# Attention's output kept by channels, and three head groups mixed at once: one change to a hybrid decoder block

## The chip, the cores and the metric

The kernel runs on one core of a Trainium2 chip. The metric is the device time of one execution in microseconds (us). The kernel before took 1356.09 us in the median of three runs, 1356.03 to 1356.96.

A core has engines with instruction rows of their own: TensorE (PE in the profile, with its weight loads as PEld), VectorE (DVE), ScalarE (ACT), GpSimd (POOL) and SyncE (SP), which here issues nearly all transfers. An engine runs its row in order, and waits on semaphores for what others have to finish first. Matmuls read the on-chip memory and write PSUM banks; ScalarE and VectorE carry PSUM out, which is called an eviction here.

## The reference

One layer of a decoder block, on 1024 positions of 1024 channels, in float32:

```python
h = rms_norm(x, mix_norm_g[layer])
proj = h @ w_in[layer]
z_a, q, k, v, gate_logits = jnp.split(proj, splits, axis=-1)
y_a = chunked_spatial_gating(gelu(z_a), ...)
...
y_b = dilated_mixture_attention(q, k, v)
gates = jax.nn.sigmoid(...)
merged = gates[:, :, 0] * (y_a @ w_branch_a) + gates[:, :, 1] * (y_b @ w_branch_b)
x = x + merged @ w_out[layer]
...
```

A convolutional gated MLP with `w_up` and `w_down` and a final norm follow. The change is in `dilated_mixture_attention`. There are three groups of four heads, 64 channels each. A group attends within a window, over every position, every 4th or every 16th. Each head gives an output and a log-sum of its exponentials for each position. The three groups are then mixed, head by head, by a softmax over the three log-sums:

```python
alpha = jax.nn.softmax(jnp.stack(lses, axis=-1), axis=-1)
mixed = jnp.einsum('bshg,bshgd->bshd', alpha, o_all)     # (1024, 256)
```

## The kernel before

**Input products.** The first long stage computes `h @ w_in` channel-major (channels on the partitions, positions along a row). It goes through 23 blocks of 256 output columns, held in `PAIRS`: three of v for the gating (zv), then for each head group, in the order 1, 2, 0, three blocks (qa, qc, v), then gate blocks ga 0 to 3, three u blocks (zu 0 to 2), and gate blocks ga 4 to 7. A block is done by seven products of half size, a scheme that trades a product for sums, in the order P1, P6, P2, P7, P5, P4, P3 (`in_order`, L326). Each product is 12 matmuls (`in_product`, L533). P2 adds into P1's PSUM bank, P4 into P7's and P3 into P5's (`SHARED`, L528). `in_evict` (L559) carries each product out: P6 at L574, P7 at L579, P5 at L581, P4 at L584 and P3 at L587, all on VectorE; P1 and P2 on ScalarE. So P4 cannot start before L579 has read P7's bank, nor P3 before L581 has read P5's.

A product's weights are raw loads (wr), summed on VectorE (L277 to L282) and split into a high part on ScalarE (L312) and a low part on VectorE (L313); `in_ahead` keeps that four products ahead and the loads nine.

**What lies between.** Small work is put between the products by a clock of ticks: `after(lag, fn)` notes a function, and `in_product` calls `tick()` after every six matmuls. TensorE's row is therefore as the code writes it. The rows of the other engines and of SP are ordered by the framework's scheduler from product 18 on, which may place an instruction earlier than the code has it; once placed, the row runs in order.

**Attention.** When a group's v block is done, `attention` (L999) turns v to position-major (`turn_v`, two 128-position transposes per block of positions), and starts eight tiles of 128 queries, five ticks apart. A tile (`Attend`, L813) loads q and k, splits them into a high and a low part (`turn`), computes scores against its own key block and, where there is one, the block before it (`score`; one block in 13 tiles, two in the other 11), takes the exponentials, transposes the probabilities (`turn_p`, pp) and multiplies them with v (`product`, pu). In before, the probabilities are the weights and 64 value channels stream past, so the output has queries on the partitions.

For groups 1 and 2 the product and its two statistics (negative maximum and denominator, four heads each) go to a scratch in DRAM, 264 numbers a row. For group 0 `combine` (L938) loads the rows of the other two, forms the three shares with a dozen small VectorE operations, scales and adds on VectorE and GpSimd, and five ticks later `turn_y` transposes the result (ybt) into YC, channel-major.

**Around it.** From zu 0 on, `wd_load` and `wd_sums` (L1060, L1068) prepare the weights of the last stage: in each of eleven steps four quarters of `w_down` are loaded, four subtractions and additions are made on VectorE (L1076), and the results are stored. There are two buffers for each quarter. In before a step comes at P1 and at P5 of each block from zu 0 on. Each zu block also multiplies u by the mixed gating values (L673). In the last block, ga 7, `y_parts` (L1080) splits the gating output ya and the attention output YC into high and low parts in R, 8 of each after P6 and 8 after P7, for the products that follow.

Of the kernel before, what the change touches and what calls it, by code (L numbers as in the profile page):

```python
# [11 lines left out]
F32 = mybir.dt.float32  # L12
# [26 lines left out]
UW = NH * HD + 2 * NH  # L39
# [55 lines left out]
def block_kernel(  # L95
# [116 lines left out]
    def after(lag, fn):  # L212
        pending.setdefault(clock[0] + lag, []).append(fn)
# [590 lines left out]

    scratch = {g: dram.tile([S, UW], F32, name=f"scr{g}") for g in (1, 2)}

# [6 lines left out]
    class Attend:  # L813
# [6 lines left out]
        def __init__(self, g, T, vts):  # L820
            self.g, self.T, self.vts = g, T, vts
# [31 lines left out]
        def score(self):  # L853
# [14 lines left out]
            st = at.tile([P, UW], F32, name=f"st_{name}", tag="st", bufs=2)  # L868
            mx = small.tile([P, NH], F32, name=f"mx_{name}", tag="mx")
            pr_t = at.tile([P, NH, 256], F32, name=f"pr_{name}", tag="pr", bufs=2)  # L870
# [23 lines left out]
            nm = st[:, 256 : 256 + NH]  # L894
            den = st[:, 256 + NH : 256 + 2 * NH]
# [6 lines left out]
            self.st, self.pr = st, pr_t  # L902
# [17 lines left out]
        def product(self):  # L920
            pu = ps_x.tile([P, 256], F32, name=f"pu_{self.name}", tag="pu")
            n = len(self.parts)
            for i, (h, s) in enumerate(self.blocks):
                vt = self.vts[self.halves[s]]
                nc.tensor.matmul(  # L925
                    pu[:, h * HD : (h + 1) * HD],
                    self.pT[:, i, :],
                    vt[:, h * HD : (h + 1) * HD],
                    start=i % n == 0,
                    stop=i % n == n - 1,  # L930
                )
            if self.g != 0:
                nc.vector.tensor_copy(self.st[:, 0:256], pu)
                nc.sync.dma_start(scratch_rows(self.g, self.T), self.st)
            else:
                self.combine(pu)

        def combine(self, pu):  # L938

            T, st = self.T, self.st  # L940
            others = []
            for g in (1, 2):
                t = at.tile([P, UW], F32, name=f"ld_{g}_{T}", tag=f"ld{g}", bufs=1)
                nc.sync.dma_start(t, scratch[g][T * P : (T + 1) * P, :])
                others.append(t)
            srcs = [st] + others
            nms = [t[:, 256 : 256 + NH] for t in srcs]
            dens = [t[:, 256 + NH : 256 + 2 * NH] for t in srcs]
            w = small.tile([P, 3, NH], F32, name=f"w_{T}", tag="w", bufs=2)
            nmin = small.tile([P, NH], F32, name=f"nmin_{T}", tag="nmin", bufs=2)  # L950
            z = small.tile([P, NH], F32, name=f"z_{T}", tag="z", bufs=2)
            wd = small.tile([P, 3, NH], F32, name=f"wd_{T}", tag="wd", bufs=2)
            nc.vector.tensor_tensor(nmin, nms[1], nms[2], ALU.min)
            nc.vector.tensor_tensor(nmin, nmin, nms[0], ALU.min)
            for g in range(3):
                nc.vector.tensor_tensor(w[:, g, :], nmin, nms[g], ALU.subtract)
            nc.scalar.activation(w, w, AF.Exp)
            for g in range(3):
                nc.vector.tensor_tensor(wd[:, g, :], w[:, g, :], dens[g], ALU.mult)
            nc.vector.tensor_tensor(z, wd[:, 0, :], wd[:, 1, :], ALU.add)  # L960
            nc.vector.tensor_tensor(z, z, wd[:, 2, :], ALU.add)
            nc.vector.reciprocal(z, z)
            zb = z.unsqueeze(1).to_broadcast([P, 3, NH])
            nc.vector.tensor_tensor(w, w, zb, ALU.mult)  # L964

            def v4(ap):
                return ap.rearrange("p (h d) -> p h d", h=NH)

            def wb(g):
                return w[:, g, :].unsqueeze(2).to_broadcast([P, NH, HD])  # L970

            yb = st[:, 0:256]
            nc.vector.tensor_tensor(v4(yb), v4(pu), wb(0), ALU.mult)
            for g in (1, 2):
                o = others[g - 1]
                nc.gpsimd.tensor_tensor(v4(o[:, 0:256]), v4(o[:, 0:256]), wb(g), ALU.mult)  # L976
                nc.gpsimd.tensor_tensor(yb, yb, o[:, 0:256], ALU.add)
            after(5, self.turn_y)

        def turn_y(self):  # L980
            pt = tr_tile(f"ybt_{self.T}")
            for c in range(2):
                nc.tensor.transpose(
                    pt[:, c * P : (c + 1) * P], self.st[:, c * P : (c + 1) * P], ident
                )
            nc.scalar.activation(
# [1525 lines left out]
```

## Time and profile before

| | before |
|---|---|
| device time, median of three runs | 1356.09 us |
| span of the profiled execution, first to last instruction | 1355.9 us |
| mean granted TensorE clock | 0.998 |
| TensorE busy | 1345.9 us, 99% |
| VectorE busy | 1038.0 us, 77% |
| ScalarE busy | 642.0 us, 47% |
| GpSimd busy | 302.2 us, 22% |
| VectorE, 420 to 440 us | 18.17 of 20 us, DMA share 0.93 |

The span and the median run are 0.2 us apart. A line of the timeline is: start, duration of the run of equal instructions, engine, line of the kernel, operation, output<-inputs, shape, count. A float32 matmul (pu, pm) is two instructions; a transpose is one. Matmuls overlap, so durations of neighbours add up to more than their starts are apart. Attention's tiles lie from about 148 to 400 us, the u blocks from about 412 us, and the gate block ga 7 ends at 545.5 us.

### The profile page before, as it was taken

To read this page: it belongs to the slowest core of one execution; us is meant where nothing else is said; L and a number is where in the kernel's file an instruction comes from. 1 tells how busy PE (TensorE), PEld (TensorE's weight loads), DVE (VectorE), ACT (ScalarE), POOL (GpSimd) and SP (SyncE) were. 2 spreads that over 40 slices of the span, in tenths; PEclk is the share of its full clock that TensorE was granted. 3 is DMA by queue.
4 is the path that set the end of the run, shared out by engine and by line. 5 is a ranking of instruction groups with operands and counts; after the bars stand their busy time and mean duration, and the time that the engine had idled before them with its cause. 6 is when DMAs were issued, how large, how long until landed. Compare 5 with 4: busy or idle time off the path is not lost.

```text
span 1355.9 us, 19084 instructions
## 1 busy us (share of the span) xinstructions
PE 1345.9 (99%) x6356; PEld 1120.5 (83%) x6356; DVE 1038.0 (77%) x1894; ACT 642.0 (47%) x1269; POOL 302.2 (22%) x302
## 2 busy tenths in 40 slices
PE   9999999999999999999999999999999999999998
PEld 8888888888888878888888888888888888888886
DVE  7988697887877988769779878666666668585674
ACT  7763455665543325435366344333433335354453
POOL 1121000001330000210010346555655553000002
PEclk9999999999999999999999999999999999999999
DMA  9435454554438994975651223333233328996663
GB/s 356 112 99 172 130 171 118 149 156 140 135 110 295 324 324 144 300 263 164 236 170 39 67 105 105 98 117 114 89 116 118 124 92 269 387 332 221 201 205 124
DMA packets 144802, 236.99 MB, mean 175 GB/s; under 512 B 13888, under 2 KB 58432, under 8 KB 144704
## 3 DMA queue, kind: packets, MB, share of 16 engines
q1 hardware_dynamic: 142464, 231.79, 51.9%
q0 software_dynamic: 1088, 2.10, 0.9%
q10 hardware_dynamic: 1152, 1.89, 0.4%
q8 instruction: 50, 0.82, 0.3%
q14 instruction: 48, 0.39, 0.1%
HBM read 167.77 MB, written 64.29 MB: 171 GB/s over the span
## 4 chain that ended last, share of the span: by engine, by line
PE 90%; DVE 4%; DMA 3%; POOL 1%; issue 1%; ACT 1%; SPq 0%; POOLq 0%; DVEq 0%; ACTq 0%
PE in_P L544 22%; PE uP L1952 21%; PE dn L2215 15%; PE up L1952 8%; PE wo_P L1784 6%; PE pa L1414 5%; PE pl L617 3%; PE pu L925 2%; PE pu L1932 2%; PE pb L1414 2%; DMA wd<-in_w_down_dram 2%; DMA wT<-wd 1%; PE pp L909 1%; DVE wd L1076 1%; DVE G L313 1%
## 5 line engine op out<-in xcount | busy, mean ns | idle before, releaser
L544 PE MATMUL in_P<-R,G 128*128 128x512 f32 x1008 | 243.8, 394 | 0.0
L544 PEld LDWEIGHTS in_P<-R,G 128*128 128x128 f32 x1008 | 185.8, 188 | 36.9
L2215 PE MATMUL dn<-R 128*128 128x512 f32 x924 | 209.6, 389 | 0.0
L2215 PEld LDWEIGHTS dn<-R 128*128 128x128 f32 x924 | 173.5, 188 | 35.9
L544 PE MATMUL in_P<-G,G 128*128 128x512 f32 x504 | 123.3, 395 | 1.4 <-DVE C L579 1.4
L170 ACT ACTIVATE R<-up 128x512 fp32r<-128x512 f32 x109 | 65.7, 622 | 123.2 <-DVE up L279 105.9
L1952 PE MATMUL uP<-G,R 128*128 128x512 f32 x504 | 121.4, 390 | 0.0
L1952 PE MATMUL uP<-R 128*128 128x512 f32 x504 | 121.2, 390 | 0.0
L312 ACT ACTIVATE G<-wr 128x512 fp32r<-128x512 f32 x126 | 78.7, 628 | 89.5 <-PE in_P L544 51.4
L1952 PE MATMUL up<-G,R 128*128 128x512 f32 x504 | 120.3, 390 | 0.0
L1952 PEld LDWEIGHTS uP<-G,R 128*128 128x128 f32 x504 | 94.5, 188 | 20.1 <-DVE R L171 0.3
L1952 PEld LDWEIGHTS up<-G,R 128*128 128x128 f32 x504 | 94.7, 188 | 19.7
L1952 PEld LDWEIGHTS uP<-R 128*128 128x128 f32 x504 | 94.7, 188 | 19.6
L544 PEld LDWEIGHTS in_P<-G,G 128*128 128x128 f32 x504 | 92.8, 188 | 21.0 <-issue 2.6
L313 DVE TENSOR_TENSOR G<-wr,G 128x512 fp32r<-128x512 f32 x126 | 88.2, 701 | 25.2 <-ACT G L312 24.3
L171 POOL TENSOR_TENSOR R<-up,R 128x512 fp32r<-128x512 f32 x55 | 73.2, 1343 | 13.1 <-ACT R L170 12.2
L170 ACT ACTIVATE R<-db 128x512 fp32r<-128x512 f32 x77 | 48.1, 626 | 55.0 <-PE dn L2215 42.7
L171 DVE TENSOR_TENSOR R<-db,R 128x512 fp32r<-128x512 f32 x77 | 53.9, 704 | 25.0 <-ACT R L170 24.9
L1414 PE MATMUL pa<-R,G 128*128 128x512 f32 x288 | 67.9, 389 | 0.0
L1414 PEld LDWEIGHTS pa<-R,G 128*128 128x128 f32 x288 | 54.1, 188 | 11.2
L544 PE MATMUL in_P<-G 128*128 128x512 f32 x252 | 61.8, 392 | 0.0
L976 POOL TENSOR_TENSOR ld<-ld,w 128x256 f32<-128x256 f32 x16 | 10.8, 696 | 228.6 <-DVE w L964 228.6
(302 smaller groups left out, 2428.2 us busy)
## 6 DMA issues: line engine op xcount, KB each, us to landing
up<-in_w_up_dram SPq DMA_DIRECT2D x44, 512.0 KB, 4.1
wr<-in_w_in_dram SPq DMA_DIRECT2D x42, 512.0 KB, 4.2
dA<-gd SPq DMA_DIRECT2D x55, 256.0 KB, 4.6
wd<-in_w_down_dram SPq DMA_DIRECT2D x44, 256.0 KB, 5.2
wT<-wd SPq DMA_DIRECT2D x44, 256.0 KB, 3.6
dS<-gS SPq DMA_DIRECT2D x44, 256.0 KB, 4.4
db<-wT SPq DMA_DIRECT2D x44, 256.0 KB, 4.5
gd<-Y SPq DMA_DIRECT2D x42, 256.0 KB, 2.0
```

What stands on the lines that cost most here:

```text
L170: nc.scalar.activation(hi, src, AF.Copy)
L171: fn = lambda: lo_eng.tensor_tensor(lo, src, f32(hi), ALU.subtract)
L312: lambda: nc.scalar.activation(op[:, 0], src, AF.Copy),
L313: lambda: nc.vector.tensor_tensor(op[:, 1], src, f32(op[:, 0]), ALU.subtract),
L544: nc.tensor.matmul(acc, op[:, w, kt, :], left[LEFT[name], kt][:, a, :], start=opened and i == 0, stop=i == len(HIGH_FIRST) - 1, skip_group ...
L617: nc.tensor.matmul(lead_banks[b][:, cs], raw_x[h, kt][:, a, c * P : (c + 1) * P], lead_op(kt, w, cs), start=kt == 0 and p == 0 and cs.star ...
L925: nc.tensor.matmul(pu[:, h * HD : (h + 1) * HD], self.pT[:, i, :], vt[:, h * HD : (h + 1) * HD], start=i % n == 0, stop=i % n == n - 1,)
L1414: nc.tensor.matmul(acc, unit[a][kt // 4][:, kt % 4, :], two(R, 8 * h + kt)[:, b, :], start=n == 0 and i == 0, stop=n == len(kts) - 1 and i ...
L1784: nc.tensor.matmul(acc, left[LEFT[name], kt][:, a, blk * P : (blk + 1) * P], out_ops[s][:, w, :], start=name not in SHARED and kt == 0 and ...
L1932: nc.tensor.matmul(acc, plain_up[which, k][:, w, kt, :], left[f"A{h + 1}{k + 1}", kt][:, a, :], start=n == 0 and i == 0, stop=n == KT - 1 ...
L1952: nc.tensor.matmul(acc, op[w][:, kt, :], left[LEFT[name], kt][:, a, :], start=opened and i == 0, stop=i == len(HIGH_FIRST) - 1, skip_group ...
L2215: nc.tensor.matmul(accs[blk], dops[s][:, 0, a, blk * P : (blk + 1) * P], dops[s][:, 1, w, :], start=SEQ[j] not in CONTINUES and kt == 0 an ...
```

## The change

The output product of attention is computed channel-major. v (64 channels of a head) is now the weights and the transposed probabilities stream past; heads 0 and 1, and 2 and 3, write partitions 0 to 63 and 64 to 127 of one bank. ScalarE copies the bank into a tile that holds a whole group, at the positions that its queries have in the sequence; for group 0 that tile is YC. Groups 1 and 2 are stored once each, when complete. Only the statistics (8 numbers a row) go through the scratch.

The product runs 13 ticks after the tile's first step instead of 10, which is the tick of the next tile's transposes and of the score two tiles on. `turn_v` turns two position blocks at once. There are fewer buffers: q and k share 2 instead of 3, probabilities have 1 instead of 2.

The shares of all tiles are formed together (`weigh`), transposed (`turn_share`, share_t), stored, and loaded again so that a share is spread over the 64 partitions of its head. `mix_groups` scales and adds the three groups in six steps of 512 positions, three ticks apart, during zu 0 and zu 1. The `w_down` steps begin at zu 2, when that memory is free, at P1, P2 and P5 of zu 2 and ga 4, and at P1 and P5 of ga 5 to 7.

```diff
-UW = NH * HD + 2 * NH
+SW = 2 * NH
...
+    def after(lag, fn, first=False):
+        due = pending.setdefault(clock[0] + lag, [])
+        due.insert(0 if first else len(due), fn)
...
-                t = at.tile([P, NH, P], F32, name=f"{o}_{self.name}", tag="qk", bufs=3)
+                t = at.tile([P, NH, P], F32, name=f"{o}_{self.name}", tag="qk", bufs=2)
...
-            pr_t = at.tile([P, NH, 256], F32, name=f"pr_{name}", tag="pr", bufs=2)
+            pr_t = at.tile([P, NH, 256], F32, name=f"pr_{name}", tag="pr", bufs=1)
...
+            for pair in range(2):
+                for k, s in enumerate(self.parts):
+                    vt = self.vts[self.halves[s]]
+                    for h in (2 * pair, 2 * pair + 1):
+                        r = h % 2 * HD
+                        nc.tensor.matmul(
+                            pu[r : r + HD, pair, :],
+                            vt[:, h * HD : (h + 1) * HD],
+                            self.pT[:, h * n + k, :],
+                            start=k == 0,
+                            stop=k == n - 1,
+                        )
+            nc.scalar.activation(self.columns(), pu, AF.Copy)
+            if self.T == NB - 1 and self.g:
+                nc.sync.dma_start(by_channel(summed_d[self.g]), self.out)
...
-            after(max(1, s - 6), self.load)
+            after(max(1, s - 4), self.load)
             after(s, self.turn)
             after(s + 3, self.score)
             after(s + 8, self.turn_p)
-            after(s + 10, self.product)
+            after(s + 13, self.product)
...
+        for T, lag in zip(range(0, 8, 2), (5, 7, 10, 12)):
+            after(lag, lambda T=T: turn_v(T), first=True)
...
+        if not g:
+            after(30, load_stats)
+            after(45, weigh)
+            after(47, turn_share, first=True)
...
+    def turn_share():
+        pt = tr_tile("share_t")
+        n = 3 * NB * NH
+        nc.tensor.transpose(pt[0:n, 0:P], share["w"], ident)
+        nc.scalar.activation(share["t"], pt[0:n, 0:P], AF.Copy)
+        nc.sync.dma_start(share_d.rearrange("c (t q) -> (c t) q", q=P), share["t"])
+
+    def mix_groups(pool):
+        shares = share_d.rearrange("(g c r) s -> g r c s", g=3, r=2)
...
+            for r in range(2):
+                nc.sync.dma_start(wb[r * HD : (r + 1) * HD], shares[g, r, :, hs].partition_broadcast(HD))
...
+        def scale(h, g):
+            wb, o = got[h, g]
+            (nc.gpsimd if g else nc.vector).tensor_tensor(o, o, wb, ALU.mult)
+
+        def add(h, g):
+            tt(got[h, 0][1], got[h, 0][1], got[h, g][1], ALU.add)
...
+        if PAIRS[n] == ("zu", 2) and name == "P1":
+            comb_stack.close()
+            wd = ya_stack.enter_context(tc.tile_pool(name="wd", bufs=2, reuse_waits="tile"))
...
-        if wd is not None and name in ("P1", "P5"):
+        if wd is not None and name in (("P1", "P5") if n > NP_IN - 4 else ("P1", "P2", "P5")):
             wd_sums(wd_step - 1)
             wd_load(wd_step)
             wd_step += 1
```

TensorE's row in group 2, before: the second tile's transposes and the third's scores, and between pieces of input products of their own the output products of the first and second tile (the numbers in a name are group and tile; in_10 is block 10).

```order
L544 MATMUL in_9_P5_2385<-G1_76 128x512 x12
L925 MATMUL pu_2_0_2480<-v_2_0_2248,pT_2_0_2432 128x64 x4
L544 MATMUL in_10_P1_2502<-R_75,G1_76 128x512 x12
L544 MATMUL in_10_P6_2518<-R_75,G1_76 128x512 x6
L909 MATMUL pp_2_1_0_2526<-ident_78,pr_2_1_2446 128x128 x4
L866 MATMUL sc_2_2_2532<-kring_1333,qs_2_2_2487 128x256 x4
L544 MATMUL in_10_P6_2518<-R_75,G1_76 128x512 x6
```

The same row with the change, one tile later: the output product of tile 2, the transposes of tile 3 and the scores of tile 4.

```order
L545 MATMUL in_10_P5_2619<-G1_76 128x512 x6
L938 MATMUL pu_2_2_2683<-pT_2_2_2590,v_2_2_2318 64x128 x4
L919 MATMUL pp_2_3_0_2690<-ident_78,pr_2_3_2604 128x128 x4
L872 MATMUL sc_2_4_2696<-kring_1336,qs_2_4_2632 128x256 x4
L545 MATMUL in_10_P5_2619<-G1_76 128x512 x6
L545 MATMUL in_11_P1_2728<-R_75,G1_76 128x512 x12
```

The output product has moved from a place of its own to the place in front of its neighbours' transposes, and is 64 rows by 128 instead of 128 by 64.

VectorE's row in the last gate block (block 22), before: the splits of R, and the evictions of P6, P7 and P5.

```order
L171 TENSOR_TENSOR R_75<-ya_4196,R_75 128x512
L574 TENSOR_TENSOR C1_104<-C1_104,in_22_P6_5142 128x512
L171 TENSOR_TENSOR R_75<-ya_4196,R_75 128x512
L171 TENSOR_TENSOR R_75<-YC_101,R_75 128x512 x2
L313 TENSOR_TENSOR G1_76<-wr_22_0_4956,G1_76 128x512
L171 TENSOR_TENSOR R_75<-ya_4196,R_75 128x512 x2
L313 TENSOR_TENSOR G1_76<-wr_22_1_4974,G1_76 128x512
L171 TENSOR_TENSOR R_75<-ya_4196,R_75 128x512
L579 TENSOR_TENSOR C1_104<-C1_104,in_22_P7_5191 128x512
L171 TENSOR_TENSOR R_75<-ya_4196,R_75 128x512 x3
L171 TENSOR_TENSOR R_75<-YC_101,R_75 128x512 x2
L581 TENSOR_TENSOR C1_104<-C1_104,in_22_P5_5221 128x512
```

With the change, from the first subtraction of the ninth `w_down` step (counted from 0) to the eviction of P5.

```order
L1124 TENSOR_TENSOR wd11_9_4850<-wd11_9_4850,wd01_9_4846 128x512
L171 TENSOR_TENSOR R_75<-ya_3947,R_75 128x512
L1124 TENSOR_TENSOR wd01_9_4846<-wd01_9_4846,wd00_9_4844 128x512
...
L1124 TENSOR_TENSOR wd10_9_4848<-wd10_9_4848,wd00_9_4844 128x512
L575 TENSOR_TENSOR C1_104<-C1_104,in_22_P6_4928 128x512
L171 TENSOR_TENSOR R_75<-ya_3947,R_75 128x512 x4
L171 TENSOR_TENSOR R_75<-YC_101,R_75 128x512 x2
L314 TENSOR_TENSOR G1_76<-wr_22_0_4718,G1_76 128x512
L314 TENSOR_TENSOR G1_76<-wr_22_1_4736,G1_76 128x512
L580 TENSOR_TENSOR C1_104<-C1_104,in_22_P7_4977 128x512
L171 TENSOR_TENSOR R_75<-ya_3947,R_75 128x512 x6
L171 TENSOR_TENSOR R_75<-YC_101,R_75 128x512 x2
L582 TENSOR_TENSOR C1_104<-C1_104,in_22_P5_5007 128x512
```

The four subtractions stand ahead of six splits that were ahead of them in before, and eight splits instead of five now lie between the evictions of P7 and P5.

TensorE's row at the end of group 0, with the change: from the scores of its last tile to the transposition of the shares (share_t).

```order
L868 MATMUL sc_0_7_3745<-kring_1336,qs_0_7_3693 128x256 x8
L545 MATMUL in_15_P1_3771<-R_75,G1_76 128x512 x12
L545 MATMUL in_15_P6_3787<-R_75,G1_76 128x512 x12
L545 MATMUL in_15_P1_3771<-R_75,G1_76 128x512 x6
L1025 MATMUL share_t_3826<-ident_78,share_3794 96x128
L938 MATMUL pu_0_6_3830<-pT_0_6_3732,v_0_6_3158 64x128 x2
```

Thirty input matmuls stand between the last scores and the transposition of the shares, and the output products of tiles 6 and 7 stand behind it. In before nothing like it is there; each tile's combine is waited for by its own ybt alone.

More of the change, by code (lines that the diff above doesn't have):

```diff
@@ L802, in turned, with by_channel @@
         after(12, rope)
-    scratch = {g: dram.tile([S, UW], F32, name=f"scr{g}") for g in (1, 2)}
+    scratch = {g: dram.tile([S, SW], F32, name=f"scr{g}") for g in (1, 2)}
+    summed_d = {g: dram.tile([256, S], F32, name=f"od{g}") for g in (1, 2)}
+    share_d = dram.tile([3 * NH, S], F32, name="share")
+    def by_channel(t):
+        return t.rearrange("(c p) s -> p c s", p=P)
     def scratch_rows(g, T):
@@ L920, in product @@
         def product(self):
-            pu = ps_x.tile([P, 256], F32, name=f"pu_{self.name}", tag="pu")
+            pu = ps_x.tile([P, 2, P], F32, name=f"pu_{self.name}", tag="pu")
             n = len(self.parts)
[L923 to L986, printed above, removed]
-                YC[:, :, self.T * P : (self.T + 1) * P],
-                pt[:, 0:256].rearrange("p (c t) -> p c t", c=2),
-                AF.Copy,
-            )
+            for pair in range(2):
[10 more added lines that the diff above has]
+                        )
@@ L1004, in turn_v @@
             pt = tr_tile(f"avt_{g}_{T}")
-            for i in range(2):
-                nc.tensor.transpose(
-                    pt[:, i * P : (i + 1) * P], ct[:, i, T * P : (T + 1) * P], ident
-                )
-            vts[T] = at.tile([P, 256], F32, name=f"v_{g}_{T}", tag="vt", bufs=8)
-            nc.scalar.activation(vts[T], pt[:, :256], AF.Copy)
-        for T in range(8):
-            after(2 + T + T // 3, lambda T=T: turn_v(T))
-            Attend(g, T, vts).start(4 + 5 * T)
-    at = kring = mask = mask2 = None
+            for k in range(4):
+                o = (T + k // 2) * P
+                nc.tensor.transpose(pt[:, k * P : (k + 1) * P], ct[:, k % 2, o : o + P], ident)
@@ new lines, in turn_v @@
+            vt = at.tile([P, 2, 256], F32, name=f"v_{g}_{T}", tag="vt", bufs=4)
+            nc.scalar.activation(vt, pt.rearrange("p (t c) -> p t c", t=2), AF.Copy)
+            vts[T], vts[T + 1] = vt[:, 0], vt[:, 1]
+        for T, lag in zip(range(0, 8, 2), (5, 7, 10, 12)):
+            after(lag, lambda T=T: turn_v(T), first=True)
+        out = at.tile([P, 2, S], F32, name=f"o_{g}", tag="o", bufs=1) if g else YC
+        for T in range(8):
+            Attend(g, T, vts, out).start(4 + 5 * T)
@@ L1018, in open_attention @@
+    at = kring = mask = mask2 = stats = None
     def open_attention():
-        nonlocal at, kring, mask, mask2
+        nonlocal at, kring, mask, mask2, stats
         at = at_stack.enter_context(tc.tile_pool(name="at", bufs=2, reuse_waits="tile"))
@@ L1116, in prep_b @@
             wunits[dt] = (his, los)
-    at_stack, zv_stack, ya_stack = ExitStack(), ExitStack(), ExitStack()
+    at_stack, zv_stack, ya_stack, comb_stack = (ExitStack() for _ in range(4))
     ps_x_stack = ExitStack()
```

81 lines of the change are left out of this document (71 added, 10 removed).

## Prediction

> **What bounds the kernel now.** I read the page first, then who TensorE waited for, then the chain of waits, then the timeline of TensorE where the change works.
>
> ```profile
> span 1355.9 us, 19084 instructions
> PE 1345.9 (99%) x6356; PEld 1120.5 (83%) x6356; DVE 1038.0 (77%) x1894; ACT 642.0 (47%) x1269; POOL 302.2 (22%) x302
> PE warm L395 <- POOL ident masks.py:199: 1.7, 1, 1.7
> PE in_P L544 <- DVE C L579: 1.4, 3, 0.9
> 482.87 62.85 PE in_P L544 x276
> ```
>
> TensorE is busy for 99% of the span and waits for anybody only twice: 1.7 us at the start and 1.4 us, in three pieces, for VectorE's eviction L579. So whatever the change takes out of TensorE's own row of instructions comes off the span in full, unless another engine makes TensorE wait anew. One undisturbed input product costs 62.85/276 = 0.228 us a matmul, 2.73 us for twelve, 19.1 us for a block of seven products. The measured median of 1356.09 us is 0.2 us above this span, so I work on the span and add 0.2. A change under 0.2% (2.7 us) is what a measurement of this kernel can hardly tell from none.
>
> Attention's small matmuls stand between pieces of the input products. Here is one tile of a group without a previous block, then the middle of one tile of the last group.
>
> ```profile
> 254.83 0.60 PE L909 MATMUL pp<-ident,pr 128*128 128x128 f32 x4
> ...
> 255.74 2.91 PE L544 MATMUL in_P<-R,G 128*128 128x512 f32 x12
> 258.48 1.00 PE L925 MATMUL pu<-v,pT 128*128 128x64 f32 x8
> 259.29 4.37 PE L544 MATMUL in_P<-R,G 128*128 128x512 f32 x18
> 263.50 0.60 PE L909 MATMUL pp<-ident,pr 128*128 128x128 f32 x4
> ...
> 344.59 1.89 PE L925 MATMUL pu<-v,pT 128*128 128x64 f32 x16
> 346.32 0.39 PE L983 MATMUL ybt<-ident,st 128*128 128x128 f32 x2
> 346.46 3.01 PE L544 MATMUL in_P<-G,G 128*128 128x512 f32 x12
> ...
> 382.92 1.81 PE L909 MATMUL pp<-ident,pr 128*128 128x128 f32 x8
> ```
>
> Matmuls overlap, so a group costs the time from its start to the next group's start. The output product costs 258.48 to 259.29 = 0.81 us (one key block) and 344.59 to 346.32 = 1.73 us (two). Its turn back (ybt) costs 0.14 us. The eighteen input matmuls behind pu take 263.50 - 259.29 = 4.21 us where 4.10 is due: each interruption costs 0.11 us behind it as well.
>
> **The change, part by part.**
>
> Output product channel-major. It runs on 24 tiles, 13 with one key block and 11 with two: 13 x 0.81 + 11 x 1.73 = 29.6 us. Now 64 columns of values are the weights and 128 queries stream past, two heads in the two column halves. The spatial gating of before already has that form, at L733.
>
> ```profile
> 110.69 0.44 PE L733 MATMUL pm<-wspT,V 128*64 128x128 f32 x4
> 110.96 0.39 PE L733 MATMUL pm<-wspT,C 128*64 128x128 f32 x4
> 111.28 0.94 PE L737 MATMUL pm<-wspT,C 128*128 128x128 f32 x6
> 112.05 0.60 PE L2454 MATMUL rot<-ident,YC 128*128 128x128 f32 x4
> 112.41 3.02 PE L544 MATMUL in_P<-G,G 128*128 128x512 f32 x12
> 115.26 0.39 PE L737 MATMUL pm<-wspT,V 128*128 128x128 f32 x2
> ```
>
> Eight 64-wide instructions last 110.69 to 111.28 = 0.59 us, the steady four 0.27; full-width ones last (112.05 - 111.28)/6 = 0.128 each, so two halves do go through in about the time of one. I price one block at 0.59 us, two at 0.59 + 2 x 0.27 = 1.13. Saved: 13 x 0.22 + 11 x 0.60 = 9.5 us. Leaving the 64-wide form costs 0.32 - 0.27 = 0.05 us, and that is inside the 0.59. [...]
>
> The product moves into the interruption of its neighbours' transposes and scores (the tick of score two tiles on), so 24 interruptions disappear: 24 x 0.05 to 0.11, I take 1.5 us. The turn back goes: 8 x 0.14 = 1.1, less one transpose for the shares, 1.0. Values are turned four blocks at a time instead of two.
>
> ```profile
> 239.93 0.38 PE L1006 MATMUL avt<-ident,C 128*128 128x128 f32 x2
> 240.07 3.02 PE L544 MATMUL in_P<-G,G 128*128 128x512 f32 x12
> 242.93 0.38 PE L1006 MATMUL avt<-ident,C 128*128 128x128 f32 x2
> ```
>
> Two cost 0.14 + (2.86 - 2.73) = 0.27 us; four, by rot above, 0.36 + (2.85 - 2.73) = 0.48. So 24 x 0.27 - 12 x 0.48 = 0.7; some shared an interruption anyway, I take 0.5. Sum of TensorE's part: 9.5 + 1.5 + 1.0 + 0.5 = 12.5 us; with the bounds, 10 to 16.
>
> Combine leaves the tiles. The eight combines waited on VectorE for their scratch loads; one held up the scores and with them pp at 382.92, which took 1.81 us instead of the 1.04 that eight take elsewhere. That goes: 0.8. The evictions of pu move to ScalarE, 47% busy: nothing. Fewer buffers for q and k (3 to 2) and for the probabilities (2 to 1): turn cannot run before the previous score anyway, since qs has one buffer, and the loads then have a whole tile of 8.7 us (254.83 to 263.50) for the 2.9 to 7.2 us that a load lands in (row below); nothing, at worst 2.
>
> The one share step. TensorE stops at share_t until the shares are made. Between the last score and it stand 30 input matmuls, 6.8 us. The path:
>
> ```profile
> L884 DVE CUSTOM_DVE_ANT_0 pr<-sc,mask 128x256 f32<-128x256 f32 x44 | 16.0, 418 | 0.3 <-PE sc L862 0.3
> L898 ACT ACTIVATE pr<-pr,st 128x256 f32<-128x256 f32 x44 | 21.8, 497 | 3.4 <-DVE st L896 3.4
> 398.34 0.16 DVE L953 TENSOR_TENSOR nmin<-ld,ld 128x4 f32<-128x4 f32 x1 [2.18 <-DMA ld<-scr]
> 400.33 0.69 DVE L313 TENSOR_TENSOR G<-wr,G 128x512 fp32r<-128x512 f32 x1
> ```
>
> Four maxima 4 x 0.42 = 1.7, four exponentials 4 x 0.50 = 2.0, a weighing as a combine's 398.34 to 400.33 = 2.0, and one to three other instructions of 0.6 us in the queues: 6.3 to 7.5 us. New wait: 0 to 0.7; with a late queue 2.5. I take 0.7. Behind it queue the products and every input matmul.
>
> The mixing itself (2 scales and 4 adds on VectorE, 4 multiplies on GpSimd, 16 loads) lies in the first two u blocks, which lose the w_down work that stood there; nobody needs YC before the last gate block. Nothing, as long as VectorE has that room: about 6 x 1.2 us in, twelve subtractions of 0.6 out.
>
> The w_down sums now begin at the third u block: the same eleven steps of four subtractions in fewer blocks, three steps in two of them. VectorE's row there, and its wait for a load:
>
> ```profile
> 420.00:440.00 20.00, 19.63 (x87) 15.99 (x86) 18.17 (x30) 7.08 (x12) 0.00 (x0) 1.00 0.93 307
> DVE wd L1076 <- DMA wd<-in_w_down_dram: 9.5, 7, 2.3
> DMA to landing us min/median/max: 2.9/5.2/7.2
> wT<-wd SPq DMA_DIRECT2D x44, 256.0 KB, 3.6
> 507.68 0.69 DVE L587 TENSOR_TENSOR C<-C,in_P 128x512 f32<-128x512 f32 x1 [0.58 <-PE in_P L544]
> 511.52 0.69 DVE L1076 TENSOR_TENSOR wd<-wd,wd 128x512 f32<-128x512 f32 x1 [1.70 <-DMA wd<-in_w_down_dram]
> 537.86 0.69 DVE L579 TENSOR_TENSOR C<-C,in_P 128x512 f32<-128x512 f32 x1
> 538.45 1.90 DVE L171 TENSOR_TENSOR R<-ya,R 128x512 fp32r<-128x512 f32 x3
> 540.26 1.29 DVE L171 TENSOR_TENSOR R<-YC,R 128x512 fp32r<-128x512 f32 x2
> 541.46 0.69 DVE L581 TENSOR_TENSOR C<-C,in_P 128x512 f32<-128x512 f32 x1
> 542.84 2.88 PE L544 MATMUL in_P<-G 128*128 128x512 f32 x12
> ```
>
> VectorE was already busy 18.17 us of 20 here and the DMA engines 93%; operations follow each other every 0.60 us (three from 538.45 take until 540.26). An eviction that comes late holds TensorE, because P4 adds into P7's bank and P3 into P5's. Third u block and fourth gate block: steps that share a buffer are joined by sum 0.6, store 3.6 and load 5.2 us, 9.4 in all, and load 4 leaves only behind the stores of step 2, so sums 4 stand waiting ahead of L580's eviction (before's L579). The old waits of 1.4 us go; in their place I put 1.5, between 0 and 4.
>
> Last gate block. Eight subtractions come in, four of them ahead of the splits of R. I count from the block's start: C(P3) and a split end at 1.4; the ninth step's loads land at 511.52 - 507.68 = 3.8 us by the row of the block before; seven operations, C(P6), eight more, C(P7): 17 x 0.6, done at 14.0, with P4 due at 13.7; eight splits and C(P5) follow, done at 19.4, where P3 is due at 16.4 (16.7 with P4's delay). In before the same eviction ended at 542.15 with P3 at 542.84. New wait about 3.0 us; 0.7 with the loads there in time, 5 with loads landing at 7.2. I take 3.0.
>
> Sum: -12.5 - 0.8 - 1.4 + 0.7 + 1.5 + 3.0 = -9.5. 1355.9 - 9.5 + 0.2 = 1346.6 us.
>
> **Rivals.**
> No new wait. The loads land early, the queues keep up: the 5.2 us of new waits shrink to 1: 1342.4. For it: two steps of w_down are loaded ahead, during the second u block, when the mixing is over. Against: the fullness of VectorE's row.
> More waiting than that. The order puts sums ahead of evictions at every step, and TensorE's clock can fall in a long stop:
>
> ```profile
> 1340.00:1350.00 10.00, 9.18 (x41) 7.28 (x39) 4.81 (x11) 4.42 (x11) 1.65 (x3) 1.00 0.26 99
> 1350.00:1356.00 6.00, 0.00 (x0) 0.00 (x0) 1.86 (x5) 1.31 (x5) 0.98 (x2) 0.59 0.52 185
> ```
>
> When TensorE stops for good the granted clock goes from 1.00 to 0.59 within the last 6 us; a stop of 3 us, then two or three microseconds at a lower clock, and waits at their upper ends (2.5 + 4 + 5) give 1355.9 - 14.7 + 11.5 + 2.5 + 0.2 = 1355.4; halfway 1351. [...]
> Slower: the w_down loads set the pace. With every landing at its longest, load and store, two steps in a shared pair of buffers take 7.2 + 4 x 0.6 + 7.2 + 1 of issue = 17.8 us, 8.9 a step. From the last add of the mixing, early in the second u block, to the last gate block there are about 105 us for eleven steps, 9.5 a step, so this does not bind. At 11.5 us a step it takes 126, 21 us too many, and 1342.4 + 21 = 1363. It outweighs the gain from 10.8 us a step. For it: 93% DMA share; against: before's loads never took longer than 7.2.
> Slower: the halves do not overlap. If the 64-wide matmuls of different tiles cost 0.128 each as L737's, pu costs 13 x 1.03 + 11 x 2.05 = 35.9 us, 6.3 more instead of 9.5 less: 1346.6 + 15.8 = 1362.4. L733's rows speak against it.
>
> **How the numbers follow.** Forecast (1343.5 to 1350) 0.52. No new wait (1339 to 1343.5) 0.22. More waiting (1350 to 1358.8) 0.18. The two slower ones 0.05 and 0.03. Under 1353.4 lie the first two and half of the third: faster 0.83; same 0.09; slower 0.08. The range leaves out the far end of more TensorE saving, the upper third of more waiting and the slower cases: 1340 to 1353.
>
> **What would show it.** Of the profile after: pu rows of the form 128*64 128x128, eight in about 0.6 us, ahead of pp and sc in one interruption; no ybt, no pp over 1.1 us; TensorE's list of waits with share_t under 1 us, and the evictions of P7 and P5 with about 4.5 us together, most of it in the last gate block. Wrong: pu eight in 0.8 or more; waits of TensorE over 10 us in all; or waits for q, k or probabilities in attention, which I priced at nothing.

## The result and the profile after

The change took 1358.93 us in the median of 14 runs (1355.48 to 1362.84), before 1356.47 in the same runs (1354.72 to 1358.44). The ratio is 1.0018, 95% interval 1.001 to 1.0025: slower by 2.4 us, where 9.5 us less was forecast. The profiled execution of the change has a span of 1359.0 us and took 1360.94, 2.0 us more than the median. One execution of a later kernel (the mixing's loads issued by GpSimd) took 3474 us, which nothing here explains and which its ratio leaves out.

The page of the kernel after, and whom TensorE waited for (us in total, times, longest):

```profile
span 1359.0 us, 18869 instructions
PE 1339.5 (99%) x6341; PEld 1104.0 (81%) x6341; DVE 1023.6 (75%) x1794; ACT 649.3 (48%) x1267; POOL 285.7 (21%) x274
PE in_P L545 <- DVE C L582: 4.5, 3, 2.5
PE in_P L545 <- DVE C L580: 3.7, 3, 2.9
PE share_t L1025 <- DVE share L1020: 1.9, 1, 1.9
PE warm L396 <- POOL ident masks.py:199: 1.7, 1, 1.7
PE in_P L545 <- ACT C L573: 0.6, 1, 0.6
```

TensorE is busy for 6.4 us less than before, and the span is 3.1 us longer. New waits make 10.7 us (4.5 + 3.7 + 1.9 + 0.6) where 1.4 stood and 5.2 were forecast. Some 5 us of the gain in busy time is hidden in matmuls that ran at half clock, as the windows below show. First the gain: TensorE's row in group 0, with the product (pu), transposes and scores in one interruption.

```profile
372.42 1.09 PE L938 MATMUL pu<-pT,v 128*64 128x128 f32 x16
373.45 1.09 PE L919 MATMUL pp<-ident,pr 128*128 128x128 f32 x8
374.30 1.20 PE L868 MATMUL sc<-kring,qs 128*128 128x256 f32 x8
375.34 2.00 PE L545 MATMUL in_P<-R,G 128*128 128x512 f32 x8
```

Sixteen instructions, two blocks, cost 373.45 - 372.42 = 1.03 us against 1.73 before; 1.13 was forecast. pp takes 1.09, not 1.81.

Three pairs of windows show what the new waits did. The columns are the length, busy time and count of PE, PEld, DVE, ACT and POOL, the granted clock, the DMA share and GB/s.

```profile
381.60:385.00 3.40, 1.50 (x15) 0.95 (x15) 2.41 (x10) 0.31 (x2) 0.00 (x0) 1.00 0.25 34
385.00:388.40 3.40, 3.40 (x20) 2.92 (x17) 0.58 (x1) 0.98 (x2) 0.00 (x0) 0.51 0.38 140
436.20:439.60 3.40, 1.24 (x6) 1.06 (x7) 3.40 (x7) 0.00 (x0) 0.00 (x0) 1.00 0.92 367
439.60:443.00 3.40, 3.40 (x10) 2.62 (x9) 2.65 (x5) 1.46 (x3) 0.00 (x0) 0.51 1.01 379
519.50:522.90 3.40, 2.08 (x10) 1.43 (x9) 1.76 (x3) 0.63 (x1) 0.00 (x0) 1.00 0.76 292
522.90:526.30 3.40, 3.40 (x17) 2.82 (x16) 3.33 (x7) 0.63 (x1) 0.00 (x0) 1.00 0.92 340
```

In the first window of each pair TensorE is idle: 1.9 us at share_t, 2.2 in zu 1 (of a stop of 2.9), 1.3 in ga 6. Behind the first two the granted clock is half for 3.4 us: in zu 1 ten matmuls run where fifteen would at 0.227 us, and 1.7 us are lost. Behind the third it is not. A third fall follows a stop of 2.45 us in ga 7, at 545.5 us, 3.41 us at 0.50. So the three falls cost some 5 us on top of the waits.

The stop in zu 1, in the rows of VectorE and GpSimd and in SyncE's row of issues:

```profile
411.85 10.19 SPq L1039 DMA_DIRECT2D wb<-share  x4
...
428.13 2.39 POOL L1048 TENSOR_TENSOR ob<-ob,wb 128x1024 f32<-128x1024 f32 x1 [7.33 <-DVE G L314]
431.73 2.40 POOL L1048 TENSOR_TENSOR ob<-ob,wb 128x1024 f32<-128x1024 f32 x1 [1.21 <-DMA ob<-od]
...
430.55 1.23 DVE L1051 TENSOR_TENSOR YC<-YC,ob 128x1024 f32<-128x1024 f32 x1 [2.56 <-POOL ob L1048]
...
432.29 2.38 DVE L314 TENSOR_TENSOR G<-wr,G 128x512 fp32r<-128x512 f32 x1
...
437.54 0.67 DVE L580 TENSOR_TENSOR C<-C,in_P 128x512 f32<-128x512 f32 x1
```

SyncE's row stood for 10 us behind loads of spread shares whose buffer was in use. The multiplies on GpSimd took 2.4 us each; VectorE's add stood in its row until the first was done, and a split that takes 0.69 elsewhere took 2.38 beside the second, so L580 ran late. The wait of 2.56 us and the 1.7 by which the split was longer make 4.3, more than the stop of 2.9; the two adds of the mixing in that stretch are 2.4 us of work. So waiting is the larger part. VectorE, 400 to 440 us:

```profile
400.00:420.00 20.00, 20.00 (x90) 16.46 (x89) 13.17 (x19) 7.21 (x11) 4.00 (x2) 1.00 0.83 215
420.00:440.00 20.00, 16.51 (x71) 12.75 (x70) 16.61 (x22) 5.06 (x9) 5.59 (x3) 0.99 0.85 283
```

It was busy for 13.17 and 16.61 us of 20, less than the 13.34 and 18.17 of before.

### The profile page after: what moved, and what is told of

It is laid out like the page before. It is cut to its first block, busy times and chain, and to the rows that moved or that the text cites. A ratio compares the mean times of both kernels' runs of the same rounds, so it can differ in the third digit from the quotient of the medians.

```text
span 1359.0 us, 18869 instructions
## 1 busy us (share of the span) xinstructions
PE 1339.5 (99%) x6341; PEld 1104.0 (81%) x6341; DVE 1023.6 (75%) x1794; ACT 649.3 (48%) x1267; POOL 285.7 (21%) x274
## 4 chain that ended last, share of the span: by engine, by line
PE 87%; DVE 5%; DMA 4%; issue 2%; ACT 1%; SPq 1%; POOL 0%; POOLq 0%; DVEq 0%; ACTq 0%
PE uP L2005 21%; PE in_P L545 19%; PE dn L2268 15%; PE up L2005 8%; PE wo_P L1837 5%; PE pa L1467 5%; PE pl L618 3%; DMA wd<-in_w_down_dram 2%; PE pu L1985 2%; PE pb L1467 2%; DVE wd L1124 1%; PE pp L919 1%; PE pu L938 1%; DMA ob<-od 1%; DVE G L314 1%
## 5 line engine op out<-in xcount | busy, mean ns | idle before, releaser
L545 PE MATMUL in_P<-R,G 128*128 128x512 f32 x1008 | 238.0, 391 | 0.6 <-ACT C L573 0.6
L171 POOL TENSOR_TENSOR R<-up,R 128x512 fp32r<-128x512 f32 x55 | 73.2, 1343 | 13.5 <-ACT R L170 12.2
L1048 POOL TENSOR_TENSOR ob<-ob,wb 128x1024 f32<-128x1024 f32 x4 | 9.6, 2398 | 279.6 <-DMA ob<-od 265.8
```

The source lines that it names most:

```text
L171: fn = lambda: lo_eng.tensor_tensor(lo, src, f32(hi), ALU.subtract)
L545: nc.tensor.matmul(acc, op[:, w, kt, :], left[LEFT[name], kt][:, a, :], start=opened and i == 0, stop=i == len(HIGH_FIRST) - 1, skip_group ...
```

## The experiments

Microseconds faster or slower than before are worked out from the ratio to before's runs on the same chip (the ratio less one, times 1356.3 us); an interval is 1.0 to 1.9 us to each side, so a difference of two kernels is known to 2 or 3 us.

**The share step later.** Four ticks:

```diff
-            after(47, turn_share, first=True)
+            after(51, turn_share, first=True)
```

> The kernel with the change, and the one transposition of the shares (share_t) four ticks, 24 input matmuls or 5.4 us, later, behind the output products of tile 6. In the profile after, TensorE stopped 1.90 us at share_t, and the 3.4 us behind the stop had a granted clock of 0.5, in which TensorE loses 1.7 us. My theory (a stop costs its length and then half of 3.4 us): both go, 3.6 us less, 1355.3 us against 1358.9 of the change. Rival A (a stop costs its own length only, the clock falls for another reason): 1.9 us less, 1357.0, and a fall of the clock remains near 385 us. Rival B (the shares are stored 5.4 us later, and the loads of the mixing behind them are what stops TensorE in the second u block): that stop grows from 2.9 us towards 5, and the time is 1357 to 1359.

Measured 1356.0 us, ratio 0.9992 (0.9982 to 1.0001), 3.5 us under the change. The stop and its fall went; block ga 3 became 3.63 us shorter, as worked out. But the stop in zu 1 grew to 3.5 us, so rival B's mechanism is there too, though the time is under its 1357 to 1359. And a stop of 2.45 us in ga 7 had no fall behind it here: a stop's price is not fixed.

**Without the mixing, w_down steps as before.** `mix_groups` isn't called; the steps begin at `("zu", 0)` at P1 and P5.

> Left out: the mixing of the three groups (its loads, multiplies and adds; the attention output used is that of one group alone). The w_down steps begin at the first u block at P1 and P5 of each block, as before the change. The shares are still formed and transposed at the same tick. This is the product form with the share step alone. My theory (TensorE's part saves 12.4 us as forecast, and the whole loss lies in the share step, the mixing and the later w_down steps): 1356.5 - 12.4 - 0.8 + 3.6 for the share step = 1346.9 us, with 1.4 or so of old w_down waits kept. Rival (the product form itself saves less than the blocks of attention show, or slows what follows): 1352 or more.

Measured 1345.35, ratio 0.9919 (0.9906 to 0.9932), 11.0 us faster than before. My theory holds, the rival falls. The stop of 1.90 us at share_t stands in this profile as well, without a fall of the clock.

**The same with the share step later.**

> Left out: the mixing, and the w_down steps are where they were before the change, as in no_mix_old_wdown; the transposition of the shares four ticks later, as in share_later. What is left is attention's output product channel-major with no new wait. The prediction put TensorE's part at 12.5 us, the hold on the probabilities at 0.8 and the old waits at 1.4 us; 0.4 of those stood in no_mix_old_wdown. So 1356.4 - 12.5 - 0.8 - 1.0 = 1342.1 us if these terms were right; 1346 or more if TensorE's part was sized too high.

Measured 1343.23, ratio 0.9905 (0.9892 to 0.9917), 12.9 us faster. Whom TensorE still waited for:

```profile
PE warm L396 <- POOL ident masks.py:199: 1.7, 1, 1.7
PE in_P L545 <- DVE C L580: 0.4, 1, 0.4
```

The gain was there, 1.4 us short of the 14.3 that the expectation adds up. Attention's own part can be read from TensorE's row: from the first matmul behind group 1's blocks to the first of zu 0 before took 263.76 us (145.99 to 409.75) and this kernel 251.45 (145.98 to 397.43), 12.3 less; TensorE's part and the hold on the probabilities were forecast at 13.3. The share step costs 12.9 - 11.0 = 1.9 us here, where the profile has no fall behind it, and 3.5 in the change, where it has one.

**Without the mixing, w_down steps as in the change.**

> Left out: the mixing, as in the run with the old w_down steps; the w_down steps stay where the change has them, from the third u block on. It differs from that run only by the place of the w_down steps, and from the change only by the mixing. My theory (mixing costs about 5.2 us in the second u block, the late w_down steps about 5.4 us of waits and 1.7 us of clock in the gate blocks): 1358.9 - 5.2 = 1353.7 us, and about 7 above the run with the old steps. Rival (the late w_down steps and their transfers are the whole loss, the mixing is hidden): 1358 to 1359, 12 above the run with the old steps. Opposite rival (the mixing alone, whose delay is handed on to the w_down steps): 1347 to 1349.

Measured 1351.18, ratio 0.9958 (0.9944 to 0.9972), 5.7 us faster than before. So the later steps cost 11.0 - 5.7 = 5.3 us and the mixing 5.7 + 2.4 = 8.1: both are real, and neither is the whole. Here ga 7 had no stop, but ga 5 one of 2.8 us, with a fall of the clock. VectorE's row in ga 5:

```profile
492.86 2.14 DVE L1124 TENSOR_TENSOR wd<-wd,wd 128x512 f32<-128x512 f32 x3 [4.23 <-DMA wd<-in_w_down_dram]
...
496.13 0.68 DVE L580 TENSOR_TENSOR C<-C,in_P 128x512 f32<-128x512 f32 x1
```

Subtractions that stand ahead of L580 waited 4.23 us for their load. In ga 7 it is not a load but the order of the row. First the change, from the ninth step's first subtraction:

```profile
528.95 0.69 DVE L1124 TENSOR_TENSOR wd<-wd,wd 128x512 f32<-128x512 f32 x1 [0.87 <-DMA wd<-in_w_down_dram]
...
538.59 0.67 DVE L580 TENSOR_TENSOR C<-C,in_P 128x512 f32<-128x512 f32 x1
539.19 3.69 DVE L171 TENSOR_TENSOR R<-ya,R 128x512 fp32r<-128x512 f32 x6
542.80 1.28 DVE L171 TENSOR_TENSOR R<-YC,R 128x512 fp32r<-128x512 f32 x2
544.00 0.68 DVE L582 TENSOR_TENSOR C<-C,in_P 128x512 f32<-128x512 f32 x1
```

This run:

```profile
534.48 0.68 DVE L580 TENSOR_TENSOR C<-C,in_P 128x512 f32<-128x512 f32 x1
535.08 1.89 DVE L171 TENSOR_TENSOR R<-ya,R 128x512 fp32r<-128x512 f32 x3
536.88 1.28 DVE L171 TENSOR_TENSOR R<-YC,R 128x512 fp32r<-128x512 f32 x2
538.09 0.68 DVE L582 TENSOR_TENSOR C<-C,in_P 128x512 f32<-128x512 f32 x1
```

In the change VectorE works without a pause from 528.95 to the end of L582, and eight splits stand between L580 and L582; here it is five. In all fourteen profiles the stop before P3 in ga 7 goes with that number: none in the seven with five splits, 1.2 us in the one with six, 2.4 to 2.9 in the six with eight. Why the framework orders the row so in one kernel and not in the other, these runs do not show. It also means that the 8.1 us hold more than the mixing's own place: compared with this run, in the profile of the change zu 1 is 5.9 us longer (24.97 and 19.05), while ga 5 is 3.7 shorter, ga 6 1.6 and ga 7 4.8 longer.

**The multiplies on VectorE.** `tt(o, o, wb, ALU.mult)` for all groups.

> The kernel with the change, and the four GpSimd multiplies of the mixing made by VectorE. In the profile after, VectorE waited for those multiplies 8.4 us in three pieces, and a multiply took 2.40 us and began only when its loads had landed. If GpSimd is the cause (its 2.4 us, and what it does to VectorE meanwhile), the stop of 2.9 us in the second u block and the clock behind it go: 1358.9 - 5 + 1 = about 1354 to 1355 us. If the loads are the cause (issued late on SyncE's queue, 6 to 12 us to land), VectorE waits for the loads directly, at the multiply, and the stop stays at 2 to 4 us: 1358 to 1360 us. I hold the second for likelier.

Measured 1355.1, ratio 0.9988 (0.9979 to 0.9997), 4 us under the change. I held the loads for likelier and was mostly wrong: the idle time in zu 1 fell from 3.5 to 1.9 us with no fall. The rest this run does not part: VectorE stood 3.06 us for a loaded group and then worked without a pause until L580, with the mixing's adds and multiplies in that stretch.

**The loads of the mixing issued by GpSimd.** On top of that, `nc.gpsimd.dma_start` for wb and ob.

> The kernel with the change, the multiplies of the mixing on VectorE as in the run before, and the loads of the mixing issued by GpSimd instead of SyncE. With the multiplies on VectorE the second u block still lost 2.4 us, of which 1.9 as stops: SyncE's row stood from 411.9 to 420.5 us behind a load of spread shares that waited for its buffer, and the loads behind it (weights, gating values) with it, and VectorE waited 3.06 us for a loaded group. My theory (the row of loads is what is left of the mixing's cost): the stops in the second u block fall under 0.5 us, 1355.1 - 2 = 1353 us. Rival (VectorE has simply too much to do there: 12 operations of 1.2 us within two blocks): the stop stays at 1.5 to 2 us and the time at 1355.

Measured 1357.96 in the median of 11, ratio 1.0008 (0.9997 to 1.0019). The stops in zu 1 went, but one of 3.9 us came in zu 0, where VectorE stood:

```profile
415.50 1.22 DVE L1048 TENSOR_TENSOR ob<-ob,wb 128x1024 f32<-128x1024 f32 x1 [6.26 <-DMA ob<-od]
...
417.85 0.68 DVE L580 TENSOR_TENSOR C<-C,in_P 128x512 f32<-128x512 f32 x1
```

The load of that group, behind a spread of shares in GpSimd's row, landed late, and the multiply waited ahead of L580. The other queue moved the wait; it did not remove it. Neither theory foresaw this.

**The w_down loads ahead of the sums, three steps in each of four blocks.**

```diff
-            wd_sums(wd_step - 1)
             wd_load(wd_step)
+            wd_sums(wd_step - 1)
```

> The kernel with the change; at each w_down step the next step's loads now stand ahead of the sums and stores of the last one in SyncE's row, and there are three steps in each of zu 2, ga 4, ga 5 and ga 6, so that none falls into ga 7. Mixing as in the change. My theory (in ga 7 four subtractions ahead of the splits make the stop of 2.5 us and its clock, and elsewhere the loads leave too late): the waits in ga 4 to ga 7 fall from 5.4 us to 2, and one fall of the clock less: 1358.9 - 3.4 - 1.7 = about 1354 us. Rival (transfers are the limit: three steps a block are 6 MB in 19 us, 315 GB/s beside the weights): the waits move to ga 5 and ga 6, each 2 to 3 us, and the time stays at 1357 to 1360.

Measured 1361.17, ratio 1.0034 (1.0021 to 1.0046), 4.6 us slower than before. The rival is nearer, though not in its place: ga 4 to ga 6 had 1.2 us of stops together and ga 7 4.8, because the last loads were issued only at 522.75 us, when ga 7 had begun, so that their four subtractions stood in ga 7's row again, with eight splits behind L580; SyncE's row could not keep three steps a block. Why it could not (its issues, its waits for stores, the transfers) this run does not part.

**All four edits at once.**

> The kernel with the change and four edits: shares transposed two ticks later, multiplies of the mixing on VectorE with the loads issued by GpSimd, the six steps of the mixing four ticks apart instead of three, and the w_down loads first with three steps a block and none in ga 7. If the three places (share step, mixing, w_down steps) are the whole loss and the edits empty them, it comes near the kernel without mixing and with the old w_down steps, 1345.35, less 2.9 for the share step, plus what the denser w_down steps still cost, 1 to 3: 1344 to 1346 us, ahead of the kernel before by 10. If the transfers of w_down hold VectorE in every block: 1350 to 1354.

Measured 1355.7, ratio 0.9995 (0.9986 to 1.0004): ten short. The stop in zu 0 (2.9 us, on a multiply that waited 5.3 us, with 6.8 us at half clock behind it) came with the queue, and the w_down steps kept 5.0 us of stops in ga 4 to ga 7.

**Mixing steps four ticks apart.** So the loads went back to SyncE's row, the multiplies stayed on VectorE and the share step two ticks later.

```diff
-            after(3 + 3 * i, lambda h=h, g=g: scale(h, g))
+            after(5 + 4 * i, lambda h=h, g=g: scale(h, g))
...
-                after(6 + 3 * i, lambda h=h, g=g: add(h, g))
+                after(6 + 4 * i, lambda h=h, g=g: add(h, g))
...
-                after(4 + 3 * i, lambda i=i: load(*steps[i + 2]))
+                after(6 + 4 * i, lambda i=i: load(*steps[i + 2]))
```

> The kernel with the change, the shares transposed two ticks later, the multiplies of the mixing on VectorE, and its six steps four ticks apart instead of three, the first of them two ticks later, each load behind the add that frees its buffer; loads on SyncE's row as in the change, w_down steps as in the change. With the loads on GpSimd's queue a multiply ahead of the eviction of P7 in the first u block waited 5.3 us for its loaded group, and TensorE stopped 2.9 to 3.9 us there. My theory (VectorE's row runs in order, so a multiply that stands in it before its loads have landed holds the eviction behind it; what counts is the time from issue to use): no stop over 0.5 us in zu 0 and zu 1, none at share_t, 1355.1 of the run with the multiplies on VectorE - 2.9 - 1.9 = 1350.3 us. Rival (VectorE's own added work of 7.4 us for six adds and two multiplies and 4.9 for four more is too much for two blocks): a stop of 1.5 us or more stays in zu 1, 1352 to 1355.

Measured 1351.0, ratio 0.996 (0.9948 to 0.9972): 5.4 us faster than before and 7.8 than the change, the best whole kernel of these. Zu 0 lost nothing and share_t nothing; in zu 1 1.45 us of stops stayed, between theory and rival. What it still waits for lies mostly in w_down's blocks, the longest stop, 2.4 us, in ga 7 with its eight splits:

```profile
PE in_P L545 <- DVE C L582: 4.5, 3, 2.4
...
PE in_P L545 <- DVE C L580: 1.6, 2, 1.1
```

**The same, multiplies back on GpSimd**, adds and loads one tick later, which this run does not part from the engine.

> The kernel of mix_later_steps with the four multiplies of groups 1 and 2 back on GpSimd, and each add and load one tick later, behind the multiply of 2.4 us. In mix_later_steps VectorE makes all twelve operations of the mixing, and TensorE still stopped 1.45 us in the second u block. If only lateness counts (a multiply or an add that stands in VectorE's row before its loads have landed), taking 4.9 us of multiplies off VectorE empties the second u block: 1351.0 - 2 = 1349 us. If a GpSimd multiply itself costs VectorE (its 2.4 us against 1.23, and VectorE operations beside it that took up to 2.38 us instead of 0.69 in the profile after), the stop stays or grows to 2.5 to 3.5 us, with a fall of the clock in some executions: 1351 to 1355 us.

Measured 1354.23, ratio 0.9984 (0.9975 to 0.9993), 3.2 us slower than with VectorE. The stops in zu 1 are 3.66 us instead of 1.45. A row of each engine, and VectorE's waits for GpSimd:

```profile
434.75 2.38 POOL L1048 TENSOR_TENSOR ob<-ob,wb 128x1024 f32<-128x1024 f32 x1 [1.38 <-DVE YC L1051]
...
435.14 2.54 DVE L314 TENSOR_TENSOR G<-wr,G 128x512 fp32r<-128x512 f32 x1
```

```profile
DVE YC L1051 <- POOL ob L1048: 10.1, 3, 3.6
```

VectorE's split began 0.39 us into the multiply and ended 0.55 us behind its end (437.68 and 437.13). So beside GpSimd's multiply VectorE's split took 2.54 us instead of 0.69, 1.85 more, where the multiply on VectorE itself takes 1.22. That the split stood until the multiply had ended is my reading of these two rows; what held it no run shows.

**The w_down loads issued by GpSimd and put ahead of the sums**, in the kernel with the mixing steps four ticks apart.

> The kernel of mix_later_steps, and the w_down loads issued by GpSimd, ahead of the sums of the step before; SyncE issues only the stores. In the profile after, an issue takes SyncE 0.4 to 0.75 us, eight a step, and in zu 2 and ga 4 its row stands behind stores that wait for VectorE's sums while the next loads wait behind them. If SyncE's row makes the w_down steps late: the waits in ga 4 to ga 7 (5.4 us and a fall of the clock of 1.7 in the profile after) fall to 1 or 2, so 1350.3 - 4 to 5 = 1346 us. If the transfers themselves do (DMA share 0.9 and over), or the loads leave GpSimd more slowly: 1350 to 1355 us.

Measured 1364.49, ratio 1.0057 (1.0044 to 1.0071): 13.2 us slower than without it. TensorE stopped 6.1 us in ga 4 and 9.1 in ga 5. GpSimd's row waited for the stores of each buffer again and again, 36.0 us in 15 pieces, and VectorE stood ahead of its subtractions, 18.9 us in seven pieces for which the profile names no releaser ("issue"). That they are the loads behind GpSimd's waits is the likely reading, not shown. One of them:

```profile
504.56 1.29 DVE L1124 TENSOR_TENSOR wd<-wd,wd 128x512 f32<-128x512 f32 x2 [4.74 <-issue]
```

My theory promised a gain and there is none; but as GpSimd's row brought waits of its own, the run does not clear SyncE's row either. What holds the chain of load, sums and store in two buffers is not settled by these runs.

**A ladder of stops in the kernel before.** The eviction of P7 repeated 1, 2, 3, 3 and 4 times in five blocks:

```diff
             add(c22, c12, src, ALU.add)
+            for _ in range({("zu", 1): 1, ("zu", 2): 2, ("ga", 4): 3, ("ga", 5): 3, ("ga", 6): 4}.get(PAIRS[n], 0)):
+                add(c22, c12, src, ALU.add)
```

> The kernel before the change, with the eviction of P7 (the same sum, written again into the same place) made once more in zu 1, twice more in zu 2, three times more in ga 4 and ga 5 and four times more in ga 6. P4 cannot start before the last of them, so TensorE stops. With the operations of VectorE's row that stand between them, 3, 5, 7, 6 and 8 operations of 0.6 us lie in a time in which P5's 2.73 us hide 4.5 of them: stops of about 0, 0.5, 1.6, 1.1 and 2.3 us, 5.5 in all. My theory as the profile after gave it (a stop of 1.9 us or more is followed by 3.4 us at half clock, one of 1.3 or less is not): the clock falls surely behind the stop in ga 6, perhaps behind that in ga 4, and the time is 1356.4 + 5.5 + 1.7 to 3.4 = 1363.6 to 1365.3 us. Rival (a fall has nothing to do with the stop): no fall, 1361.9. Second rival, from the runs so far, in which a stop of 1.90 us at share_t was followed by a fall in four profiles and in one was not, and a stop of 2.84 us in ga 7 was not: whether a fall follows differs from execution to execution, and the times of this kernel scatter over some 4 us where those of before scatter over 3.

Measured 1367.54, ratio 1.008 (1.0066 to 1.0094), 11 us slower, above my range: the stops were 1.95, 2.18, 1.46 and 2.54 us, 8.1 instead of 5.5 (that of 1.95 ended on ScalarE, the others on L581, which in this kernel is the repeated eviction of P7). One fall came, behind the longest. Two pairs of windows, the stop of 2.18 us and that of 2.54:

```profile
483.40:486.80 3.40, 1.56 (x7) 1.34 (x8) 2.11 (x4) 0.38 (x1) 0.00 (x0) 1.00 1.03 391
486.80:490.20 3.40, 3.40 (x17) 2.81 (x16) 1.66 (x3) 0.63 (x1) 0.00 (x0) 1.00 0.84 289
...
524.40:527.80 3.40, 0.92 (x5) 0.42 (x3) 3.28 (x6) 0.63 (x1) 0.00 (x0) 1.00 0.01 2
527.80:531.20 3.40, 3.34 (x8) 2.69 (x9) 0.69 (x1) 0.00 (x0) 0.00 (x0) 0.50 0.21 80
```

The first stop lay from 483.06 to 485.24, across the edge of a window, so that 1.81 us of it fell into one. The second lay inside one but for 0.06 us. The first rival is refuted, since the fall came behind the longest stop and none came without one; so is my theory, since the stops of 1.95 and 2.18 us had no fall behind them. The length alone does not decide.

## Why the prediction was wrong, point by point

- **TensorE's part, the hold on the probabilities and the old waits (-14.7 together): nearly right.** With the new waits taken away, and 0.4 us of old ones left, the kernel was 12.9 us faster. The upper bound of 16 for TensorE's part no run shows; attention's own part, with the hold on the probabilities, came to 12.3.
- **The share step (+0.7): too small.** A stop of 1.9 us in the profile; in time 1.9 without a fall of the clock, 3.5 with it. The chain was longer than the 6.3 to 7.5 us: from the scores' end, where the row of 375.34 begins, to the end of the last share operation at 384.08 it took 8.7. VectorE lost 2.48 us of it, standing behind a split whose high part ScalarE made late:

```profile
377.75 0.46 DVE L1012 TENSOR_TENSOR share<-share,stats 128x32 f32<-128x32 f32 x3
380.69 0.69 DVE L314 TENSOR_TENSOR G<-wr,G 128x512 fp32r<-128x512 f32 x1 [2.48 <-ACT G L313]
...
383.62 0.46 DVE L1020 TENSOR_TENSOR share<-share 128x32 f32<-128x32 f32 x3
```

- **The w_down steps (+1.5 and +3.0): nearly the size, 5.3.** The working put 3.0 on ga 7's order, and in the profile of the change that is what came, on the eviction that was named: 0.27 us on L580 and 2.45 on L582, behind eight splits. In the blocks before it the stops were 2.6 us, up to 1.3 each, where 1.5 was forecast; there VectorE waited for w_down's loads, 8.6 us in five pieces with ga 7's 0.87. But the order is not the same in every kernel, and the fall of the clock behind ga 7's stop was not priced.
- **The mixing (0): the step that failed.** The prediction put "Nothing, as long as VectorE has that room: about 6 x 1.2 us in, twelve subtractions of 0.6 out." VectorE had the room, and stood in it: in zu 1 its row stood 2.56 us at one add. Operations were counted; the waits in front of them (loads of ob in 5.8 to 12.2 us, GpSimd's 2.4 us, VectorE's split of 2.38 beside it) were not, though evictions that TensorE waits for stand behind them. It cost 8.1 us by the difference of the kernels, of which 5.9 show in zu 1.
- **The price of a stop: its length alone.** The falling clock was left to the rival of more waiting, as one block of 2.5 us behind a stop of 3 us, a price that no run shows. In the profiled execution there were three falls, 1.7 us each, behind stops of 1.90, 2.88 and 2.45 us.
- **The sum.** -12.9 + 1.9 + 5.3 + 8.1 = +2.4. That this is what the change measured is no proof: the terms are differences of neighbouring kernels and add up by construction, and taken in another order they would split otherwise. Against the forecast of -9.5 the gain was 1.8 us smaller, and the share step 1.2, the w_down steps 0.8 and the mixing 8.1 dearer. The time lies at the far end of the rival of more waiting, which had the nearest mechanism, 11.5 us of waits and a falling clock; but it built them from the share step and w_down alone. The two slower rivals named w_down's loads as the pace and the halves; the halves do overlap (sixteen instructions in 1.03 us), the loads cost about their forecast, and no rival named the mixing. Of the signs given, "waits of TensorE over 10 us in all" was the one that came.

## What to carry to other kernels

Work that is moved onto an engine with room is free only if it is ready when its turn comes: for each operation ask what it waits for, how long before its use that is issued, and which urgent instruction stands behind it. Where the row has no pause, count what stands between two urgent instructions, too: three splits more between two evictions went with a stop of 2.4 us here. A gain on the bounding engine is first had alone (here by leaving the new work out), and each new wait is then priced against it. And a stop of TensorE can cost more than its length: that of 1.90 us at share_t cost 3.5 with a fall of the clock behind it, 1.9 without.

## What the hardware showed that was not expected

In the profile after the falls of the clock stand on a grid. They begin at 385.03, 439.65, 545.46 and, at the end, 1354.42 us. The trace's record of the granted clock gives each of the first three 3.413 us at 0.5, and the four beginnings lie 16, 31 and 237 such steps apart. TensorE was idle for 1.90, 2.13 and 2.45 us of the step ahead of the first three falls, and for 1.01 us of the step with the stop in ga 6, which had none behind it. With such a grid laid in each of the fourteen profiles by its own fall at the end, I summed TensorE's idle time in each step. Each of the 18 falls before the end came behind a step with 1.86 us idle or more; of the steps with 1.1 to 1.85, twenty, none had one behind it; one with 1.90 had none, in the first run without the mixing. A fall lasted one step, or two (three times) where the stop reached into the next. In ga 7 a stop of 2.43 us across an edge (multiplies back on GpSimd) made the block 22.03 us long, one of 2.42 us inside a step (mixing steps four ticks apart) 23.52; undisturbed it takes 19.04. The grid does not lie alike in all profiles: the ladder's fall, at 527.8 us, stands 0.6 us off the steps of the profile after. That it lies anew in each execution of one kernel, and the falls with it, is likely, not shown; the change's times do scatter with the granted clock: 1355.5 and 1356.3 us at 0.998, 1360.1 and 1362.8 at 0.994.
